# Experts: chosen tokens fetched by an indirect DMA, results added in place, weight rows dealt out in pairs, one more lasting place for weights

## Chip, cores and metric

One core of a Trainium2 chip runs the whole program. The metric is the device time of one execution in microseconds (us), the median of several runs. The profile comes from one further execution, and all rows below are of that one.

## What is computed

Two transformer blocks run one after the other on 512 tokens of width 1024. The change is about the experts at the end of the first block: 16 experts, each taking the 64 tokens that it rates highest, with three 1024x1024 float32 weight matrices per expert.

```python
def expert_choice_moe(h, w_router, w_gate, w_up, w_down):
    b_, length, _ = h.shape
    cap = EC_CAPACITY_FACTOR * length // N_EXPERTS          # 64
    aff = jax.nn.softmax((h @ w_router).astype(jnp.float32), axis=-1)
    gate, idx = lax.top_k(jnp.swapaxes(aff, 1, 2), cap)
    xe = h[bidx, idx]
    hid = jax.nn.silu(jnp.einsum("becd,edf->becf", xe, w_gate)) * jnp.einsum("becd,edf->becf", xe, w_up)
    ye = jnp.einsum("becf,efd->becd", hid, w_down) * gate[..., None].astype(h.dtype)
    return jnp.zeros_like(h).at[bidx, idx].add(ye)
...
x = x + g1 * y_x                                            # the token mixer's result
x = x + g2 * expert_choice_moe(modulate(rms_norm(x, norm2_g[l]), sh2, sc2), ...)
```

## The kernel before

The program is one stream per engine, laid out ahead of time by a scheduler: the order of the instructions on each engine is fixed, and an engine waits in order on semaphores.

The token mixer ends in `mix_out`, which adds its result to `X` (512 tokens as 4 blocks of 128 partitions, 1024 columns) and computes the router's logits. `router` makes the affinities `aff` and, for each expert, the place 1 to 64 of each chosen token (`sl`, 0 where it isn't chosen). `moe` then goes through 8 rounds `p`, two experts in each, one in each half of the 128 partitions:

- `prep(p)` fetches the chosen tokens by matrix multiplication. A one-hot matrix `D` of the 512 tokens by 128 places is made (L1069) and scaled by the tokens' rms factor (L1080); for each of 8 column chunks four matmuls of X by D (L1085) give the tokens already transposed, and ScalarE and VectorE scale and shift them into `xe` (L1087, L1090).
- three products, `G` (gate), `U` (up) and `Y` (down), of 32 matmuls each, 64 columns of the array for each expert (L1063; L1051 in the last round, where `gemm_parts` makes Y in three pieces of columns).
- between U and Y the hidden values `hs` are multiplied (L1128), transposed (`tp`, L1130) and copied to `hT` (`xh` in the profile, L1131, L1132).
- `back(p)` transposes a second one-hot D (L1099) to `oh` and picks the gate values with four matmuls (L1104).
- Y is scaled to `ye` (part of the tile `hy`, L1153) and split in a high and a low half `yh` (L1154, L1155); for each of 4 token blocks and 2 column pieces two matmuls (L1158, L1159) spread it back over the tokens, and VectorE adds that to `ACC` (L1164). In the last round X, to which GpSimd has added ACC (L1151), takes the sum.

The weights come in pieces of 1 MiB: two rows blocks of 128, for each partition two runs of 1024 floats, so 4 KB each. `mload` hands out places for them in a fixed cycle: 6 of kind x1, 3 raw, 3 hl (two halves of 512 KB), 3 x2. Before that cycle, 6 further places serve once (four in `rw1`, `rw2`, and two that become ACC afterwards): 21 pieces can be there when the first round begins. The transfers are issued by SyncE's queue (SP) in the order of use, and each waits until the matmuls on the piece that had its place are done. 192 pieces are needed in all. The last 8 pieces (12 transfers, in `gemm_parts`) have a list of their own: three places x2 and one of `rw2`, three times over.

```python
todo = (kinds[:6] + [(self.rw1, "rw2"), (self.rw2, "rw")] + kinds[6:] +
        [(self.rw1, "rw"), (self.rw2, "rw2")] + acc)
```

Of the kernel before, what the change touches and what calls it, by code (L numbers as in the profile page):

```python
# [20 lines left out]
def constants():  # L21
# [31 lines left out]
    iota = np.repeat(np.arange(1, 65, dtype=f)[None, :], 128, axis=0)  # L53
    return {
# [6 lines left out]
    }  # L61


class Build:
# [111 lines left out]
    def first_mixer(self):  # L176
# [32 lines left out]
        put("n2", I["norm2_g"][0].rearrange("(r p) -> r p", p=128), 8)  # L209
        put("lb", I["hg_lb_logits"].rearrange("a b (h p) -> (a b h) p", p=128), 16)  # L210
        put("hgn", I["hg_norm_g"][0].rearrange("(r p) -> r p", p=128), 4)
        self.prow = rows
# [9 lines left out]
        nc.vector.tensor_copy(self.pcol, tp[:, :128])  # L222
        cs = p1.tile([128, 8, 32], F32, name="cs")
# [157 lines left out]
        es1.close()  # L381
        esw = ExitStack()
# [20 lines left out]
    def ctx_part(self, cx, rest):  # L403
# [20 lines left out]
        def shift(i):  # L424
            for j, at in enumerate((0, 1, 2, 3)):
                if at == i:
                    self.mod_col(cx, pc, (self.sh2, self.sc2)[j // 2], 3 + j // 2, j % 2)
# [18 lines left out]
        nc.vector.scalar_tensor_tensor(self.sc2, self.sc2, 1.0, self.c("n2"), op0=ALU.add, op1=ALU.mult)  # L446
# [458 lines left out]
    def mod_col(self, pool, psp, out, wi, half, tag="mr"):  # L905

        nc = self.nc
        for s, row in self.mod_rows(pool, psp, wi, tag, (half,)):
            ps = psp.tile([128, 512], F32, name="mr", tag=tag, bufs=self.nmr)
            for k in range(4):  # L910
                nc.tensor.matmul(ps[:, 2 * k:2 * k + 2], row[:, k * 128:(k + 1) * 128], self.selc,
                                 start=True, stop=True)
            c = 8 * wi + 4 * s
            nc.vector.tensor_tensor(out[:, 4 * s:4 * s + 4], ps[:, :8].rearrange("p (k i) -> p k i", i=2)[:, :, 0],
                                    self.c("bmod")[:, c:c + 4], op=ALU.add)

    def mix_out(self, end):
# [3 lines left out]
        nc.sync.dma_start(wr, I["w_router"][0].rearrange("(k p) e -> p k e", p=128))  # L921
# [9 lines left out]
        def logits(n):  # L931
            for k in (2 * n, 2 * n + 1):
                tp = pp.tile([128, 512], F32, name="tp", tag="tp", bufs=2)
                for b in range(4):
                    nc.tensor.transpose(tp[:, b * 128:(b + 1) * 128], self.X[:, b, k * 128:(k + 1) * 128], self.ident)
# [26 lines left out]
    def router(self):  # L962

        nc, mo, ms, pp = self.nc, self.mo, self.ms, self.pmx
        iota = self.iota = ms.tile([128, 64], F32, name="iota")
        nc.sync.dma_start(iota, self.I["k_iota"])
        rs = self.rs = ms.tile([128, 4], F32, name="rs")
# [3 lines left out]
        e = self.aff = ms.tile([128, 4, 16], F32, name="aff")  # L971
# [32 lines left out]
    def moe(self):  # L1004
# [7 lines left out]
        todo = (kinds[:6] + [(self.rw1, "rw2"), (self.rw2, "rw")] + kinds[6:] +  # L1012
                [(self.rw1, "rw"), (self.rw2, "rw2")] + acc)

        def mload(src, last):
            if last == 2 and not self.tail:

                self.tail = True
                todo[:] = ["x2", "x2", "x2", (self.rw2, "rw2")] * 3
            if not todo:  # L1020
                todo.extend(k for k in kinds if not last or k != "hl")
            kind = todo.pop(0)
            shape = [128, src.shape[1], src.shape[2]]
# [12 lines left out]
            else:  # L1036
                pool, n = (self.mwx, 6) if kind == "x1" else (ms, 3)
                t = pool.tile(shape, F32, name="mwt", tag="mwt", bufs=n)
# [3 lines left out]
        def gemm_parts(ps, lhs, wa, wb):  # L1042

            ws = [w.rearrange("(k p) f -> p k f", p=128) for w in (wa, wb)]
            for y, c in zip(ps, parts):
                for kk in range(2):
                    tl = [mload(w[:, 4 * kk:4 * kk + 4, c], 2) for w in ws]
# [6 lines left out]
        def gemm(ps, lhs, wa, wb, last=0):  # L1054
            wa = wa.rearrange("(k p) f -> p k f", p=128)
            wb = wb.rearrange("(k p) f -> p k f", p=128)
            for kk in range(4):
                tl = [mload(w[:, 2 * kk:2 * kk + 2, :], last) for w in (wa, wb)]
# [8 lines left out]
        def onehot(p, tag, prev=None):  # L1067
            D = ms.tile([128, 4, 128], F32, name="D", tag=tag, bufs=1)
            ins = nc.vector.tensor_tensor(D.rearrange("p b (a s) -> p b a s", a=2),  # L1069
                                          self.iota.unsqueeze(1).unsqueeze(1).to_broadcast([128, 4, 2, 64]),  # L1070
                                          self.sl[:, :, 2 * p:2 * p + 2].unsqueeze(3).to_broadcast([128, 4, 2, 64]),
                                          op=ALU.is_equal)
            if prev:
                self.after(ins, prev)
            return D

        def prep(p):

            Ds = onehot(p, "Ds")
            nc.vector.tensor_tensor(Ds, Ds, self.rs.unsqueeze(2).to_broadcast([128, 4, 128]), op=ALU.mult)  # L1080
            xe = XE[p % 2]
            for k in range(8):
                ps = self.psmm()[:, :128]
                for b in range(4):
                    nc.tensor.matmul(ps, self.X[:, b, k * 128:(k + 1) * 128], Ds[:, b], start=(b == 0), stop=(b == 3))  # L1085
                if k % 2:
                    nc.scalar.activation(xe[:, k], ps, AF.Identity, bias=self.sh2[:, k:k + 1],  # L1087
                                         scale=self.sc2[:, k:k + 1])
                else:
                    ins = nc.vector.tensor_scalar(xe[:, k], ps, self.sc2[:, k:k + 1], self.sh2[:, k:k + 1],  # L1090
                                                  op0=ALU.mult, op1=ALU.add)
            return xe, ins

        def back(p, prev):

            D = onehot(p, "D", prev)
# [3 lines left out]
            oh = ms.tile([128, 512], F32R, name="oh", tag="oh", bufs=1)  # L1100
            nc.scalar.activation(oh, ps, AF.Copy)
            gps = self.psmm()
            for b in range(4):
                nc.tensor.matmul(gps[:, :16], D[:, b], self.aff[:, b], start=(b == 0), stop=(b == 3))  # L1104
            gc = ms.tile([128, 1], F32, name="gc", tag="gc", bufs=2)
            for a in range(2):
                nc.vector.tensor_copy(gc[64 * a:64 * a + 64], gps[64 * a:64 * a + 64, 2 * p + a:2 * p + a + 1])
            return oh, gc
# [3 lines left out]
        xe, ins = prep(0)  # L1112
        for p in range(8):
# [3 lines left out]
            if p == 0:  # L1117
# [3 lines left out]
                hs, ye = hy[:, 0], hy[:, 1]  # L1121
            nc.scalar.activation(hs, G, AF.Silu)
            U = pg.tile([128, 2, 512], F32, name="U", tag="gu", bufs=2)
            gemm(U, xe, wu[2 * p], wu[2 * p + 1], int(p == 7))
            oh, gc = back(p, ins)
            if p < 7:
                xe, ins = prep(p + 1)
            nc.vector.tensor_tensor(hs, hs, U, op=ALU.mult)  # L1128
            for k in range(8):
                nc.tensor.transpose(tp[:, k], hs[:, k * 128:(k + 1) * 128], self.ident)  # L1130
# [14 lines left out]
            yh = self.rw1.tile([128, 2, 1024], F32R, name="yh", tag="rw")  # L1145
            if p == 0:
                ACC = [pl.tile([128, 2, 1024], F32, name="acc", tag=t) for pl, t in acc]
                ACC = [ACC[b // 2][:, b % 2] for b in range(4)]
            elif p == 7:
                for b in range(4):  # L1150
                    nc.gpsimd.tensor_tensor(self.X[:, b], self.X[:, b], ACC[b], op=ALU.add)  # L1151
            for y, s in zip(Y, parts):
                nc.vector.scalar_tensor_tensor(ye[:, s], y, gc, self.g2[:, s], op0=ALU.mult, op1=ALU.mult)  # L1153
                nc.scalar.activation(yh[:, 0, s], ye[:, s], AF.Copy)  # L1154
                nc.vector.tensor_tensor(yh[:, 1, s], ye[:, s], yh[:, 0, s], op=ALU.subtract)  # L1155
                for b in range(4):
                    ps = self.psmm()[:, :s.stop - s.start]
                    nc.tensor.matmul(ps, oh[:, b * 128:(b + 1) * 128], yh[:, 1, s], start=True, stop=False)  # L1158
                    nc.tensor.matmul(ps, oh[:, b * 128:(b + 1) * 128], yh[:, 0, s], start=False, stop=True)  # L1159
                    if p == 0:  # L1160
                        nc.vector.tensor_copy(ACC[b][:, s], ps)
                    else:
                        d = ACC[b][:, s] if p < 7 else self.X[:, b, s]
                        nc.vector.tensor_tensor(d, ps, d, op=ALU.add)  # L1164
# [503 lines left out]
```

## Time and profile before

| what | value |
|---|---|
| median of three runs | 1828.63 us (1821.88 to 1828.9) |
| the profiled execution, its own time | 1826.09 us |
| its span, first to last instruction | 1824.3 us |
| mean granted TensorE clock | 0.975 of 2.4 GHz |
| TensorE (PE) busy | 1718.1 us, 94% |
| VectorE, ScalarE, GpSimd busy | 46%, 35%, 11% |
| moved from and to memory | 327.76 MB, 180 GB/s on average |

A busy share is an average over stages with different limits, so the table only tells that TensorE is seldom idle. "Busy" for matmuls is modelled from their pipelining. The experts run from about 637 us to 1151 us; the rows of that stretch are given further below.

### The profile page before, as it was taken

Reading aid. Unit: us, or ns where it says so; the run is one execution under the profiler, and the core shown is the slowest. Engines: PE = TensorE matmul, PEld = TensorE weight load, DVE = VectorE, ACT = ScalarE, POOL = GpSimd, SP = SyncE. Lnnn points to the kernel's source line nnn. Section 1 sums busy time; section 2 is a strip of 40 time slices with the busy share of each in tenths; the row PEclk is TensorE's granted clock in tenths of the full one; section 3 lists DMA queues with packets and bytes.
Section 4 is the critical chain, followed back from the end, with each engine's and each line's share of the span. In section 5 each row is a group of like instructions: output and inputs, shape, how many; then the busy total and the mean of one; then the engine's idle time right before and its main releaser. Section 6 shows DMA issues by size and latency. Waiting matters only on the chain.

```text
span 1824.3 us, 26988 instructions
## 1 busy us (share of the span) xinstructions
PE 1718.1 (94%) x11159; PEld 1251.9 (69%) x11159; DVE 842.7 (46%) x1613; ACT 631.1 (35%) x1098; POOL 198.3 (11%) x225
## 2 busy tenths in 40 slices
PE   5998888999999599999999999899999999999999
PEld 3986768776778553444334333697667989898989
DVE  5637898856334512212212221656774543434342
ACT  4627675566323210010000000555563241324131
POOL 0103343122110000000000001410221000000000
PEclk9999898999999799999999999999999999999999
DMA  9562111211568578999999996441002223323231
GB/s 309 181 210 70 48 47 43 70 36 35 211 215 300 189 291 324 407 409 380 395 373 364 407 386 229 140 162 47 24 24 70 73 90 93 107 78 116 70 116 47
DMA packets 177395, 327.76 MB, mean 180 GB/s; under 512 B 8580, under 2 KB 115816, under 8 KB 177272
## 3 DMA queue, kind: packets, MB, share of 16 engines
q1 hardware_dynamic: 176480, 325.44, 49.4%
q8 instruction: 88, 1.44, 0.3%
q10 hardware_dynamic: 744, 0.51, 0.1%
q14 instruction: 35, 0.29, 0.0%
q0 software_dynamic: 48, 0.08, 0.0%
HBM read 323.91 MB, written 2.10 MB: 179 GB/s over the span
## 4 chain that ended last, share of the span: by engine, by line
PE 63%; DVE 4%; ACT 1%; DMA 1%; issue 1%; POOL 0%; SPq 0%; DVEq 0%; ACTq 0%
PE mm L85 10%; PE mm L84 10%; PE mm L86 10%; PE G L1063 7%; PE U L1063 6%; PE Y L1063 5%; PE mm L1085 3%; PE po L1595 1%; PE mm L1158 1%; PE pt L1548 1%; PE mm L1159 1%; PE sc L1527 1%; PE sc L1528 1%; PE Y L1051 1%; PE hp L1450 0%
## 5 line engine op out<-in xcount | busy, mean ns | idle before, releaser
L76 ACT ACTIVATE whi<-wraw 128x1024 fp32r<-128x1024 f32 (+1 forms) x171 | 173.3, 1017 | 364.7 <-PE mm L84 176.8
L78 DVE TENSOR_TENSOR wlo<-wraw,whi 128x1024 fp32r<-128x1024 f32 (+1 forms) x171 | 208.1, 1218 | 122.4 <-ACT whi L76 121.6
L85 PE MATMUL mm<-whi,ul 128*128 128x256 f32 x512 | 144.3, 282 | 0.0
L84 PE MATMUL mm<-wlo,uh 128*128 128x256 f32 x512 | 143.2, 281 | 0.0
L86 PE MATMUL mm<-whi,uh 128*128 128x256 f32 x512 | 143.2, 281 | 0.0
L84 PE MATMUL mm<-HXl,whi 128*128 128x512 f32 x256 | 106.5, 416 | 0.0
L85 PE MATMUL mm<-HXh,wlo 128*128 128x512 f32 x256 | 105.4, 412 | 0.1
L86 PE MATMUL mm<-HXh,whi 128*128 128x512 f32 x256 | 105.2, 411 | 0.0
L84 PE MATMUL mm<-H,whi 128*128 128x512 f32 x256 | 99.7, 390 | 0.0
L86 PE MATMUL mm<-H,whi 128*128 128x512 f32 x256 | 99.7, 389 | 0.0
L85 PE MATMUL mm<-H,wlo 128*128 128x512 f32 x256 | 99.6, 389 | 0.0
L85 PEld LDWEIGHTS mm<-whi,ul 128*128 128x128 f32 x512 | 96.5, 188 | 1.0 <-DVE ul L1631 0.8
L84 PEld LDWEIGHTS mm<-wlo,uh 128*128 128x128 f32 x512 | 96.2, 188 | 0.2
L86 PEld LDWEIGHTS mm<-whi,uh 128*128 128x128 f32 x512 | 96.2, 188 | 0.0
L1085 PEld LDWEIGHTS mm<-D,X 128*128 128x128 f32 x512 | 61.8, 199 | 18.5 <-issue 15.4
L1640 DVE SCALAR_TENSOR_TENSOR X<-mm,r,X 128x256 f32<-128x256 f32 x64 | 30.9, 482 | 88.2 <-PE mm L86 88.2
L1085 PE MATMUL mm<-D,X 128*128 128x128 f32 x512 | 66.6, 287 | 2.8 <-DVE D L1080 1.8
L1151 POOL TENSOR_TENSOR X<-X,acc 128x1024 f32<-128x1024 f32 x4 | 9.3, 2364 | 533.6 <-issue 533.6
L1128 DVE TENSOR_TENSOR hy<-hy,U 128x1024 f32<-128x1024 f32 x8 | 9.8, 1221 | 124.4 <-PE U L1063 124.4
L1063 PE MATMUL Y<-mwt,xh 128*64 128x512 f32 x240 | 60.0, 594 | 5.4 <-DVE xh L1131 5.4
L1626 DVE TENSOR_SCALAR r<-mm 128x512 f32<-128x512 f32 x32 | 22.1, 691 | 85.3 <-PE mm L86 85.3
L1153 DVE SCALAR_TENSOR_TENSOR hy<-Y,gc,g 128x512 f32<-128x512 f32 (+1 forms) x17 | 11.6, 716 | 107.0 <-PE Y L1063 100.1
(541 smaller groups left out, 4180.0 us busy)
## 6 DMA issues: line engine op xcount, KB each, us to landing
mwt<-in_w_exp_gate_dram SPq DMA_DIRECT2D x41, 1024.0 KB, 8.9
mwt<-in_w_exp_up_dram SPq DMA_DIRECT2D x35, 1024.0 KB, 10.2
mwt<-in_w_exp_down_dram SPq DMA_DIRECT2D x33, 1024.0 KB, 12.4
wraw<-in_w_in_dram SPq DMA_DIRECT2D x29, 1024.0 KB, 6.6
wraw<-in_w_mod_dram SPq DMA_DIRECT2D x16, 1024.0 KB, 6.9
wraw<-in_w_up_dram SPq DMA_DIRECT2D x16, 1024.0 KB, 5.5
wraw<-in_w_down_dram SPq DMA_DIRECT2D x16, 1024.0 KB, 5.0
mwh<-in_w_exp_up_dram SPq DMA_DIRECT2D x30, 512.0 KB, 9.4
```

Of the source, the lines that this page charges most:

```text
L76: i1 = self.nc.scalar.activation(hi, src, AF.Copy)
L78: i2 = self.nc.vector.tensor_tensor(lo, src, hi, op=ALU.subtract)
L84: mm(ps, ah, bl, start=first, stop=False)
L85: mm(ps, al, bh, start=False, stop=False)
L86: mm(ps, ah, bh, start=False, stop=last)
L1051: nc.tensor.matmul(y[64 * a:64 * a + 64], lhs[:, k, 64 * a:64 * a + 64], tl[a][k4], start=(k == 0), stop=(k == 7))
L1063: nc.tensor.matmul(ps[64 * a:64 * a + 64, n], lhs[:, k, 64 * a:64 * a + 64], tl[a][k2][:, n * 512:(n + 1) * 512], start=(k == 0), stop=(k ...
L1085: nc.tensor.matmul(ps, self.X[:, b, k * 128:(k + 1) * 128], Ds[:, b], start=(b == 0), stop=(b == 3))
L1158: nc.tensor.matmul(ps, oh[:, b * 128:(b + 1) * 128], yh[:, 1, s], start=True, stop=False)
L1159: nc.tensor.matmul(ps, oh[:, b * 128:(b + 1) * 128], yh[:, 0, s], start=False, stop=True)
L1626: nc.vector.tensor_scalar(r, ps, 0.0, None, op0=ALU.max)
L1640: nc.vector.scalar_tensor_tensor(self.X[:, b, s], ps, r2[:, b:b + 1], self.X[:, b, s], op0=ALU.mult, op1=ALU.add)
```

## The change

Five things change in the experts, and their neighbours follow.

1. The sum of the mixer, X, is also written to memory (`XD`, in 4 pieces, on GpSimd's queue). For each round, `chosen(p)` multiplies the one-hot D by `aff`, which has two more columns now: the token's number and its rms factor. An indirect DMA on GpSimd's queue fetches the 128 rows of XD into `xg` (the first) or into `ye`, half of the tile `hy` (the other seven). `prep(p)` scales them (128x1024) and turns them by 8 transposes.
2. ACC is gone: the results are added to X directly. Rounds 0 and 1, 2 and 3, 4 and 5 are spread back together, with four matmuls in a row in one accumulation, so 8 additions for two rounds.
3. Weight rows are dealt out to the partitions in pairs: a partition holds rows 2p and 2p+1 of a block of 256, one run of 8 KB. The columns of X, `xg` and `hs` are taken with a step of 2 where they are transposed (`chunk`), and the per-column vectors (router, shift, scale) are loaded to match; for that, three small loads and two small transposes come in at the start of the program (`r256`, `pair`).
4. The cycle has one more lasting place, x3, so 16; the two that became ACC are gone, so 20 pieces can be there at the beginning.
5. The last 8 pieces have nine places instead of four: five of x1's six, x2's three, and one of `rw2`; each of their tiles comes in two transfers.

```diff
+def chunk(k):
+    return slice(k // 2 * 256 + k % 2, k // 2 * 256 + 256, 2)
...
+        for i, src in enumerate((I["b_mod"][0, 3072:4096], I["b_mod"][0, 4096:5120], I["norm2_g"][0])):
+            nc.scalar.dma_start(r256[4 * i:4 * i + 4], src.rearrange("(r p) -> r p", p=256))
...
+                if b == 3:
+                    nc.gpsimd.dma_start(self.XD.rearrange("(b p) f -> p b f", p=128)[:, :, s], self.X[:, :, s])
...
+        nc.gpsimd.tensor_copy(self.aff[:, :, 16], iota[:, 64:])
+        nc.gpsimd.tensor_copy(self.aff[:, :, 17], rs)
...
-        acc = [(self.mwx2, "acc0"), (self.mwx2, "acc1")]
-        kinds = ["x1"] * 6 + ["raw"] * self.nraw + ["hl"] * (self.nhl // 2) + ["x2"] * 3
+        kinds = ["x1"] * 6 + ["raw"] * self.nraw + ["hl"] * (self.nhl // 2) + ["x2"] * 3 + ["x3"]
+        place = {"x1": (self.mwx, "mwt", 6), "x2": (ms, "mwt", 3), "x3": (self.mwx2, "mwt", 1)}
...
-                todo[:] = ["x2", "x2", "x2", (self.rw2, "rw2")] * 3
+                todo[:] = ["x1", "x1", (self.rw2, "rw2"), "x2", "x2", "x2", "x1", "x1", "x1", "x1",
+                           (self.rw2, "rw2"), "x2"]
...
-            wa = wa.rearrange("(k p) f -> p k f", p=128)
-            wb = wb.rearrange("(k p) f -> p k f", p=128)
+            ws = [w.rearrange("(k p j) f -> p k j f", p=128, j=2) for w in (wa, wb)]
...
+        def chosen(p, xg):
+            D = onehot(p, "D")
+            ps = self.psmm()[:, :18]
+            for b in range(4):
+                nc.tensor.matmul(ps, D[:, b], self.aff[:, b], start=(b == 0), stop=(b == 3))
+            g = ms.tile([128, 18], F32, name="gs", tag="gs", bufs=2)
+            nc.vector.tensor_copy(g, ps)
+            at = ms.tile([128, 1], U32, name="at", tag="at", bufs=2)
+            nc.vector.tensor_copy(at, g[:, 16:17])
+            nc.gpsimd.indirect_dma_start(xg, None, self.XD, bass.IndirectOffsetOnAxis(ap=at, axis=0))
+            return xg, g
...
+        def prep(p, xg, g):
+            nc.vector.tensor_scalar(xg, xg, g[:, 17:18], None, op0=ALU.mult)
             xe = XE[p % 2]
-            for k in range(8):
-                ps = self.psmm()[:, :128]
-                for b in range(4):
-                    nc.tensor.matmul(ps, self.X[:, b, k * 128:(k + 1) * 128], Ds[:, b], start=(b == 0), stop=(b == 3))
+            for k0 in range(0, 8, 4):
+                ps = self.psmm()
+                for k in range(k0, k0 + 4):
+                    nc.tensor.transpose(ps[:, (k - k0) * 128:(k - k0 + 1) * 128], xg[:, chunk(k)], self.ident)
...
-        xe, ins = prep(0)
+        ch = chosen(0, ms.tile([128, 2, 1024], F32, name="xg", tag="rw")[:, 0])
+        xe = prep(0, *ch)
+        held = []
...
+            if p < 7:
+                ch = chosen(p + 1, ye)
...
-            yh = self.rw1.tile([128, 2, 1024], F32R, name="yh", tag="rw")
-            if p == 0:
-                ACC = [pl.tile([128, 2, 1024], F32, name="acc", tag=t) for pl, t in acc]
-                ACC = [ACC[b // 2][:, b % 2] for b in range(4)]
-            elif p == 7:
-                for b in range(4):
-                    nc.gpsimd.tensor_tensor(self.X[:, b], self.X[:, b], ACC[b], op=ALU.add)
+            yh = (ms if p % 2 else self.rw1).tile([128, 2, 1024], F32R, name="yh", tag="rw")
+            held.append((oh, yh))
...
+                if p in (0, 2, 4):
+                    continue
...
+                    parts_ = [(o, y[:, i, s]) for o, y in held for i in (1, 0)]
+                    for i, (o, v) in enumerate(parts_):
+                        nc.tensor.matmul(ps, o[:, b * 128:(b + 1) * 128], v, start=(i == 0), stop=(i == len(parts_) - 1))
+                    nc.vector.tensor_tensor(self.X[:, b, s], ps, self.X[:, b, s], op=ALU.add)
```

The scheduler places the new steps. On TensorE before, from the first U to the first Y (one-hot transposes L1099, gate values L1104, the fetch L1085, transposes of hs L1130):

```order
L1063 MATMUL U<-mwt,xe 64x512 x8
L1099 MATMUL mm<-ca,D 128x128 x4
L1104 MATMUL mm<-aff,D 128x16 x4
L1085 MATMUL mm<-D,X 128x128 x32
L1130 MATMUL tp<-ca,hy 128x128 x8
```

The same place now (L1148 one-hot transposes, L1132 transposes of the fetched tokens, L1181 those of hs, L1117 the matmuls of `chosen` for round 2; those for round 1 stand ahead of U):

```order
L1100 MATMUL U<-mwt,xe 64x512 x8
L1148 MATMUL mm<-ca,D 128x128 x4
L1132 MATMUL mm<-ca,hy 128x128 x8
L1181 MATMUL tp<-ca,hy 128x128 x8
L1117 MATMUL mm<-aff,D 128x18 x4
```

The 32 matmuls of the fetch have become 8 transposes, and the gate values have moved into `chosen`.

On TensorE now, the G of round 2, which stands for those of rounds 4 and 6 (L1209 spreads rounds 0 and 1 back, L1117 is `chosen` for round 3, L1132 the transposes of its tokens):

```order
L1100 MATMUL G<-mwt,xe 64x512
L1209 MATMUL mm<-yh,oh 128x512 x28
L1100 MATMUL G<-mwt,xe 64x512 x16
L1117 MATMUL mm<-aff,D 128x18 x4
L1148 MATMUL mm<-ca,D 128x128
L1100 MATMUL G<-mwt,xe 64x512 x7
L1148 MATMUL mm<-ca,D 128x128 x3
L1100 MATMUL G<-mwt,xe 64x512
L1132 MATMUL mm<-ca,hy 128x128 x8
L1100 MATMUL G<-mwt,xe 64x512 x7
```

Between the choice of the tokens and the transposes that need them stand 8 matmuls of G and 4 transposes.

On VectorE now, from the end of round 2 into round 3, which stands for rounds 4 and 5 as well (L1200 makes `ye` in the tile hy, L1202 its low half, L1127 scales the tokens that the indirect DMA has brought into hy):

```order
L1182 COPY xh<-tp 128x512
L1200 SCALAR_TENSOR_TENSOR hy<-Y,gc,g_4734 128x512 x2
L1202 TENSOR_TENSOR yh<-hy,yh 128x512
L1178 COPY gc<-gs 64x1 x2
L1202 TENSOR_TENSOR yh<-hy,yh 128x512
L1127 TENSOR_SCALAR hy<-hy,gs 128x1024
L1139 TENSOR_SCALAR xe<-mm,sc_695,sh_694 128x128 x4
```

The tokens of the next even round land in the tile that Y's result has just left, so their fetch waits for the end of Y and L1202.

## Rows read from the trace of the kernel before

**Rows 1.** Busy time by stretch: us, PE, PEld, DVE, ACT, POOL, clock, DMA share, GB/s.

```profile
687.28:745.55 58.27, 57.00 (x293) 25.71 (x293) 13.58 (x23) 5.28 (x9) 0.00 (x0) 1.00 0.89 342
...
939.04:1003.85 64.81, 61.70 (x292) 26.28 (x292) 13.61 (x23) 5.17 (x9) 0.00 (x0) 1.00 0.96 377
```

**Rows 2.** What SP's transfers waited for, 480 to 1160 us, the longest total.

```profile
SPq L1039 <- PE G L1063: 105.0, 34, 15.0
```

**Rows 3.** Chain that ended last, one early round and parts of later ones.

```profile
687.28 13.95 PE Y L1063 x64
...
720.93 13.73 PE U L1063 x63
735.25 0.80 PE mm L1104 x8
736.05 6.48 PE mm L1085 x56
...
869.95 15.53 PE Y L1063 x64
...
1000.70 1.23 DVE hy L1128
1001.98 1.11 PE tp L1130 x8
1003.11 0.70 DVE xh L1131
```

**Rows 4.** Chain that ended last, the last round.

```profile
1122.82 3.67 PE Y L1051 x16
...
1126.95 4.55 DMA mwt<-in_w_exp_down_dram
...
1138.25 6.15 DMA mwo<-in_w_exp_down_dram
...
1150.60 0.74 DVE X L1164 x2
```

**Rows 5.** Busy time by stretch: full DMA engines with runs of 4 KB and of 1 KB.

```profile
20.00:25.00 5.00, 5.00 (x45) 2.41 (x44) 3.11 (x6) 0.77 (x2) 0.00 (x0) 1.00 1.08 338
25.00:30.00 5.00, 4.83 (x36) 2.48 (x35) 3.66 (x8) 0.00 (x0) 0.00 (x0) 1.00 1.07 350
...
752.00:840.00 88.00, 83.91 (x410) 36.07 (x407) 21.78 (x37) 7.10 (x12) 0.00 (x0) 1.00 1.03 409
```

**Rows 6.** Costs of one: line, engine, operation, shapes, count, busy us, mean ns.

```profile
L1164 DVE TENSOR_TENSOR acc<-mm,acc 128x512 f32<-128x512 f32 x48 | 31.2, 686 | 17.3 <-PE mm L1159 17.3
...
L1154 ACT ACTIVATE yh<-hy 128x512 fp32r<-128x512 f32 x15 | 9.3, 630 | 108.6 <-DVE hy L1153 108.6
...
L1090 DVE TENSOR_SCALAR xe<-mm,sc,sh 128x128 f32<-128x128 f32 x16 | 6.6, 410 | 44.2 <-PE mm L1085 44.2
```

**Rows 7.** The only DMA on GpSimd's queue (80 KB): times in ns, then landing.

```profile
L539 POOL DMA_DIRECT2D levf<-in_k_lev_dram x1: 719/719/719, 131.1 to 131.1; - x1
...
DMA to landing us min/median/max: 5.1/5.1/5.1
```

**Rows 8.** DMA issues by kind: count, KB each, median us from issue to landing.

```profile
wraw<-in_w_exp_gate_dram SPq DMA_DIRECT2D x11, 1024.0 KB, 16.5
```

**Rows 9.** In order of time, the start: ScalarE and the wait that ends it.

```profile
8.63 1.06 ACT L256 ACTIVATE junk<-X 128x1024 f32<-128x1024 f32 x1
...
17.65 2.74 DVE L260 TENSOR_SCALAR X<-X,rs 128x1024 f32<-128x1024 f32 x4
17.68 0.18 PEld L298 LDWEIGHTS wm<-wmt,cs 128*32 128x32 f32 x2 [8.33 <-DVE rs L141]
```

**Rows 10.** In order of time, from the router to the first G.

```profile
637.30 0.69 DVE L1069 TENSOR_TENSOR D<-iota,sl 128x512 f32<-128x512 f32 x1
...
638.78 10.06 PE L1085 MATMUL mm<-D,X 128*128 128x128 f32 x64 [1.77 <-DVE D L1080]
```

**Rows 11.** A weight load's wait where the array changes between 64 and 128 columns.

```profile
PEld mm L1085 <- issue: 15.4, 19, 0.8
```

More of the change, by code (lines that the diff above doesn't have):

```diff
@@ L222, in first_mixer @@
         nc.vector.tensor_copy(self.pcol, tp[:, :128])
+        tp = pst.tile([128, 512], F32, name="tp", tag="tr", bufs=2)
+        for j in range(2):
+            nc.tensor.transpose(tp[:, 12 * j:12 * j + 12], r256[:, j::2], self.ident[:12, :12])
+        self.pair = p1.tile([128, 2, 12], F32, name="pair")
+        nc.vector.tensor_copy(self.pair, tp[:, :24].rearrange("p (j r) -> p j r", j=2))
         cs = p1.tile([128, 8, 32], F32, name="cs")
@@ L381, in first_mixer @@
         es1.close()
+        dp = self.es.enter_context(tc.tile_pool(name="xd", bufs=1, space=bass.MemoryType.DRAM))
+        self.XD = dp.tile([512, 1024], F32, name="XD")
         esw = ExitStack()
@@ L445, in ctx_part @@
         shift(3)
-        nc.vector.scalar_tensor_tensor(self.sc2, self.sc2, 1.0, self.c("n2"), op0=ALU.add, op1=ALU.mult)
+        pairs = lambda t: t.rearrange("p (k j) -> p k j", j=2)
+        nc.vector.scalar_tensor_tensor(pairs(self.sc2), pairs(self.sc2), 1.0, self.pair[:, :, 8:]
+                                       .rearrange("p j k -> p k j"), op0=ALU.add, op1=ALU.mult)
         nc.scalar.activation(KY, FR, AF.Sigmoid, scale=-1.0)
@@ L1022, in mload @@
             kind = todo.pop(0)
+            if len(src.shape) == 4:
+                pool, tag, n = kind + (None,) if isinstance(kind, tuple) else place[kind]
+                t = pool.tile([128, src.shape[1] * 2, src.shape[3]], F32, name="mwt", tag=tag, bufs=n)
+                for i in range(src.shape[1]):
+                    nc.sync.dma_start(t[:, 2 * i:2 * i + 2], src[:, i])
+                return [t[:, i] for i in range(t.shape[1])]
             shape = [128, src.shape[1], src.shape[2]]
@@ L1036, in mload @@
             else:
-                pool, n = (self.mwx, 6) if kind == "x1" else (ms, 3)
-                t = pool.tile(shape, F32, name="mwt", tag="mwt", bufs=n)
+                pool, tag, n = place[kind]
+                t = pool.tile(shape, F32, name="mwt", tag=tag, bufs=n)
                 nc.sync.dma_start(t, src)
@@ L1097, in back @@
+        def back(p):
+            D = onehot(p, "D")
             ps = self.psmm()
@@ L1099, in back @@
                 nc.tensor.transpose(ps[:, b * 128:(b + 1) * 128], D[:, b], self.ident)
-            oh = ms.tile([128, 512], F32R, name="oh", tag="oh", bufs=1)
+            oh = ms.tile([128, 512], F32R, name="oh", tag="oh", bufs=2)
             nc.scalar.activation(oh, ps, AF.Copy)
-            gps = self.psmm()
-            for b in range(4):
[L1104 to L1108, printed above, removed]
+            return oh
         wg, wu, wd = I["w_exp_gate"][0], I["w_exp_up"][0], I["w_exp_down"][0]
         XE = {0: self.xp.tile([128, 8, 128], F32, name="xe", tag="g1")}
-        xe, ins = prep(0)
+        ch = chosen(0, ms.tile([128, 2, 1024], F32, name="xg", tag="rw")[:, 0])
+        xe = prep(0, *ch)
+        held = []
         for p in range(8):
@@ L1124, in moe @@
             gemm(U, xe, wu[2 * p], wu[2 * p + 1], int(p == 7))
-            oh, gc = back(p, ins)
+            oh = back(p)
             if p < 7:
-                xe, ins = prep(p + 1)
+                xe = prep(p + 1, *ch)
+            gc = ms.tile([128, 1], F32, name="gc", tag="gc", bufs=2)
+            for a in range(2):
+                nc.vector.tensor_copy(gc[64 * a:64 * a + 64], gs[64 * a:64 * a + 64, 2 * p + a:2 * p + a + 1])
             nc.vector.tensor_tensor(hs, hs, U, op=ALU.mult)
             for k in range(8):
-                nc.tensor.transpose(tp[:, k], hs[:, k * 128:(k + 1) * 128], self.ident)
+                nc.tensor.transpose(tp[:, k], hs[:, chunk(k)], self.ident)
             nc.vector.tensor_copy(hT[:, 0:4], tp[:, 0:4])
```

83 lines of the change are left out of this document (40 added, 43 removed).

## The prediction

> **What bounds the kernel now.** I read the windows of the expert stretch first, one for each round from the start of a Y to the next Y. An early round takes 58.27 us and a late one 64.81 us, with TensorE busy 57.00 and 61.70 us of them, while the DMA engines stand at a share of 0.89 and 0.96 [rows 1]. So two limits lie side by side: TensorE's stream of work, and 24 MiB of weights for a round. Which of them gives way is told by the queue's own waits: the transfers on SP waited most of all for TensorE to be done with a place, 105.0 us for G alone [rows 2]. TensorE sets the pace, and the weights keep up with little to spare. The chain of waits agrees: through the rounds it runs over TensorE, with VectorE between U and Y [rows 3], and only in the last round over transfers, 4.55 and 6.15 us [rows 4]. From the first G (its fetch begins at 638.78 us and takes 10.06 us [rows 10], so 648.8) to the last addition to X (1150.60 + 0.74 [rows 4], so 1151.3) it is 502.5 us. I work out this stretch anew on both limits and take the longer.
>
> **TensorE's time, term by term.** I start from the early round of [rows 3], whose order of work is that of the new round 0.
>
> Products: G, U and Y keep their matmuls, 13.95 us for Y and 13.73 us for U [rows 3]; I take 13.75 for each of G and U.
>
> Fetch: U ends at 720.93 + 13.73 = 734.66 us and the next Y starts at 745.55 us [rows 1, 3], so 10.9 us between them. Of it the fetch itself is 6.48 us and the gate values 0.80 us [rows 3]. Now 8 transposes stand there; the 8 of hs take 1.11 us [rows 3]. What is left on the path is VectorE's: the product of hs 1.23 us, three scalings at 0.41 [rows 6], a one-hot 0.69 [rows 10], the copy 0.70 [rows 3], together 3.85, with hand-overs 4.1 us. In a late round, where the fetch stands elsewhere, U to Y is 1.23 + 1.11 + 0.70 with hand-overs 3.2 us [rows 3].
>
> Spreading back: from the end of Y (687.28 + 13.95 = 701.23) to the start of U (720.93) it is 19.7 us [rows 3]; less G that is 6.0 us, some 5.5 without the hand-over at U. Two rounds together need as many matmuls as before but half the additions: 8 of 0.69 us [rows 6] hide behind 32 matmuls of some 0.23 us, 7.4 us; ahead of them TensorE waits for the first yh (two steps of VectorE of 0.69 and one of ScalarE of 0.63 us [rows 6], less one matmul of G, 1.7 us). So 9.5 us for two rounds instead of 11.
>
> Changes of the array: in rounds 2 to 6 the transposes and `chosen` stand among the matmuls of G in three places. A weight load waited up to 0.8 us at each such change [rows 11]; three make 2.4 us in a round.
>
> The wait for the indirect DMA is the new term. No row shows one. The only DMA on GpSimd's queue landed 5.1 us after its issue with 80 KB [rows 7]. 512 KB take 1.3 us at 409 GB/s [rows 5], and 2.6 us if half the engines' time goes to the weights; I take 5.1 + 2.6 = 7.7 us. The bounds are 3.2 us shorter (at 4.5 us: the same landing without its 0.72 us of issue, nothing for the bytes) and, from the rows of weight transfers beside it, a median landing of up to 16.5 us [rows 8]. It is nearer the first, since the engine's queue is its own. Rounds 0 and 1 have all of U between choice and use, and hide it. In G of rounds 2, 4 and 6, 8 matmuls of G (3.4 us) and 4 transposes lie between: copy, one-hot and cast 1.1 us, landing 7.7, scaling 0.69 us (2.74 us for four [rows 9]) make 9.5 us, against some 4.5: a wait of 5 us, three times. In G of rounds 3 and 5 the fetch waits for Y's result to leave the tile hy (four steps of VectorE of 0.69 us as in [rows 6], two short copies and the hand-overs, 3.7 us), so its tokens are ready 3.7 + 7.7 + 0.7 = 12.1 us after Y; TensorE has 9 matmuls of G, 3.9 us: a wait of 8.2 us, twice. After the wait for the late Y the clock fell and its 64 rows took 15.53 us instead of 13.95 [rows 3]; I add 2 us to each of these two.
>
> The stretches: first G to first Y 13.9 + 2 (G now starts on an array that has rested, where the fetch used to come first) + 0.9 + 13.75 + 4.1 = 34.7. Round 0 to 1: 13.95 + 13.75 + 13.75 + 4.1 + 0.8 = 46.4. A late round without spreading: 13.95 + 27.5 + 3.2 + 0.55 for the one-hot + 0.8 + 1.1 + 2.4 = 49.6. Rounds ending on pairs: 49.6 + 9.5 + 5 = 64.1, three times; those between: 49.6 + 8.2 + 2 = 59.8, twice; the last but one, with a spread of its own and no fetch: 49.6 - 2.7 + 5.5 = 52.4. The last round took 1151.3 - 1122.8 = 28.5 us with 10.7 us of waits for transfers [rows 4], which the nine places remove if the queue never stands: 17.8. Sum 34.7 + 46.4 + 192.3 + 119.6 + 52.4 + 17.8 = 463 us.
>
> **The weights' time.** Full engines moved 409 GB/s with runs of 4 KB and 338 to 350 with runs of 1 KB [rows 5]: 160 ns and 47.6 ns for a run on one of 16 engines. The line through both gives 310 ns for 8 KB, 423 GB/s. I take that; the bounds are 409 (nothing) and 424. After 20 pieces that are there, 164 follow before the last eight: 134 in runs of 8 KB at 2.48 us, 30 of kind hl still in 4 KB at 2.56, seven fetches at 1.28, and the last 8 in runs of 2 and 1 KB, 23 us: 332 + 77 + 9 + 23 = 441. With 4 us until the first place is free and 6 from the last landing to the last addition it is 451 us, and 462 at 409 GB/s.
>
> A rule of the Trainium skill speaks against the long runs: "DMA: Bandwidth & Descriptors", Why small descriptors are slow, puts the overhead at about 3 bus cycles for a packet. By it an 8 KB run saves some 1% on 4 KB (an estimate from that page), 414 GB/s, and the weights' path would be 458 us. The two rates of [rows 5] show a dearer packet than that.
>
> So TensorE's 463 us is the longer by a little: a gain of 39.5 us in the stretch.
>
> **What lies around.** At the start ScalarE's second square, 1.06 us and 0.19 to read it [rows 9], now stands behind the exponential, and TensorE was waiting there for what follows it, 8.33 us [rows 9]: 1.3 us lost, 0 at best. Router to first G: before 638.78 + 10.06 - 637.30 = 11.5 us [rows 10]; now one-hot 0.7, four matmuls 1.7, copy, one-hot and cast 1.1, fetch 5.1 + 1.3 (the weights' queue is quiet then), scaling 0.7, four transposes and one scaling 1.5: 12.1, so 0.6 more, I take 1. The four writes of X (2 MB, 5.1 us) lie under `mix_out` and the router, whose chain on VectorE comes before their first use; without that cover they would cost their 5 us once. Taking the tokens' columns with a step of 2 as the transposes' weights is in no row: nothing, or at most a doubled load, 1.1 us for 8 transposes, 18 us over all rounds; I take nothing, since the transposes differ in nothing else, and keep 18 for the range.
>
> 1826.1 - 39.5 + 1.3 + 1 = 1789 us against the profiled execution. The median of the runs is 2.5 us above that one: 1791.5 us.
>
> **Rivals.** (a) The weights become the bound: the fetch lands in 4.5 us, the waits fall away, and the stretch takes 451 us: 1779.5 us. For it: the DMA share of 0.96 already. Against: it needs every fetch quick. (b) The waits are longer, or the strided transposes cost part of their 18 us: 10 us of landing make 5 x 2.3 = 12 us more, both together 1805 to 1820 us. (c) Slower than before: the fetch takes its turn behind the weights already queued on the engines and lands like them, 16.5 us after its issue [rows 8]. Then five waits in G grow by 8.8 us each, rounds 0 and 1 are still covered, and TensorE stands while the places are full, so nothing is hidden: +44 us, 1835.5 us. It decides from a landing of some 15 us on. For it: SP keeps several MiB issued ahead. Against: it is another queue, and [rows 7] landed beside SP's traffic in 5.1 us. The Trainium skill, "DMA: Bandwidth & Descriptors", Queues, rings and completion order, says that an engine goes round its queues packet by packet; by that rule (c) can't be, and no row here shows it under full load. (d) No change: the change does its fetch but TensorE, freed, meets weights that move no faster and places that are fewer at the start; by the 462 us above that cannot eat more than 1 us, so it needs (b) in full and a lost tail, 10.7 us: 1830 us.
>
> **Chances.** Forecast (1782 to 1803) 0.55, (a) 0.15, (b) 0.17, (c) 0.08, (d) 0.05. Likeliest 1791.5 us. The range runs from the weights' bound at its best, with the start's 1.3 us saved, 1774, to the worst of (b) with the strided transposes, 1823; (c) and most of (d) stay out. A measurement tells 0.5% (9 us) from no change: faster 0.87, same 0.05, slower 0.08.
>
> **What the profile will show.** A round of some 47 us first, then pairs of about 64 and 60; transposes of the fetch waiting for VectorE's scaling, and that for the DMA, 5 and 8 us; landing of the fetch near 8 us; full-engine rate of 420 or more; no wait for transfers in the last round. The prediction fails if the fetch lands past 12 us, if waits for weights appear in every G, or if the 8 transposes take over 2 us.

## The result, and the profile after

The changed kernel takes 1814.19 us in the median of 4 runs (1812.67 to 1816.36), against 1828.32 us before, now also in the median of 4 runs: a ratio of 0.9932, 95% interval 0.9907 to 0.9956. It is 14 us faster where 37 had been forecast. The profiled execution has a span of 1810.9 us, 13.4 less than before.

The stretch that the prediction reckoned, from the first G to the last addition to X, went from 502.5 us to 1139.17 - 649.74 = 489.4 us, where 463 had been forecast. What lies around it changed little: the first G starts 0.9 us later (2.3 had been forecast), and what follows the experts is 1.2 us shorter. So the whole error lies in the stretch. Its windows from one Y to the next, with the same columns as [rows 1]:

```profile
649.74:683.64 33.90, 33.49 (x166) 13.55 (x168) 6.74 (x16) 6.02 (x12) 0.98 (x1) 0.97 0.84 336
683.64:728.96 45.32, 44.86 (x217) 16.46 (x218) 8.40 (x17) 4.76 (x10) 0.95 (x1) 1.00 1.02 418
728.96:800.62 71.66, 61.62 (x263) 25.48 (x263) 15.84 (x30) 6.00 (x12) 0.95 (x1) 0.95 1.02 420
800.62:861.33 60.71, 49.28 (x212) 18.66 (x213) 7.21 (x13) 4.60 (x9) 0.95 (x1) 0.92 1.01 413
861.33:930.52 69.19, 59.23 (x261) 25.26 (x261) 15.69 (x29) 5.80 (x11) 0.95 (x1) 0.98 0.98 399
930.52:991.24 60.72, 49.09 (x213) 18.66 (x213) 7.22 (x13) 4.60 (x9) 0.95 (x1) 0.92 0.99 396
991.24:1057.48 66.24, 56.50 (x248) 23.70 (x249) 14.15 (x25) 5.20 (x10) 1.26 (x9) 0.97 0.98 405
1057.48:1113.13 55.65, 51.66 (x220) 18.93 (x221) 9.93 (x14) 3.47 (x6) 0.00 (x0) 0.97 0.88 338
1113.13:1139.20 26.07, 24.13 (x144) 13.71 (x144) 10.66 (x23) 4.86 (x9) 2.53 (x2) 1.00 0.59 179
```

Column by column: in the five windows from 728.96 us on TensorE is idle for 9.7 to 11.6 us each and its clock is below full, while the DMA engines are at a share of about 1. Two limits lie side by side, as before, and the share alone can't say which one gives way. TensorE's own waits can (engine, what waited, for what: us in total, times, longest):

```profile
PE mm L1132 <- DVE hy L1127: 33.4, 5, 9.4
PE tp L1181 <- DVE hy L1179: 8.3, 6, 1.4
PE mm L1209 <- DVE yh L1202: 7.0, 5, 2.2
```

In the whole list of the matmuls' waits in this stretch no transfer of weights stands; SP's transfers, in turn, still wait for TensorE, the answer to [rows 2]:

```profile
SPq L1076 <- PE G L1100: 103.3, 25, 33.6
```

So TensorE sets the pace, and stands still for 33.4 us at the transposes of the fetched tokens. The chain of waits shows what for, in the round that begins at 728.96 us (start, us, what; the trace has two records for a matmul of G, U or Y, so x64 stands for 32 matmuls, and two for one of L1117):

```profile
728.22 0.74 PE mm L1209 x2
728.96 11.30 PE Y L1100 x50
740.26 0.66 PE mm L1209 x2
740.92 3.15 PE Y L1100 x13
...
744.56 0.74 DVE hy L1200
...
746.73 8.72 PE mm L1209 x28
755.45 7.02 PE G L1100 x32
762.47 1.01 PE mm L1117 x8
...
765.12 8.50 DMA hy<-XD,at
...
774.45 1.98 PE mm L1132 x8
776.43 4.28 PE G L1100 x14
780.72 1.00 PE mm L1117 x8
...
782.72 0.59 PE mm L1148 x4
```

The fetch, 8.5 us from issue to landing, stands in the chain between the choice (L1117) and the transposes (L1132), inside G. The median landing of the seven fetches, by the page's DMA issues (count, median us), was forecast at 7.7 us:

```profile
hy<-XD,at POOLq DMA_INDIRECT x7, 8.7
```

What the clock did around these waits (windows, columns as above):

```profile
747.00:750.00 3.00, 3.00 (x8) 1.92 (x8) 1.72 (x3) 0.00 (x0) 0.00 (x0) 0.52 1.03 429
750.00:755.00 5.00, 5.00 (x21) 3.56 (x20) 3.26 (x5) 0.00 (x0) 0.00 (x0) 0.95 1.01 419
755.00:762.00 7.00, 7.00 (x34) 2.23 (x33) 0.89 (x2) 0.00 (x0) 0.00 (x0) 1.00 1.01 417
...
774.45:776.43 1.98, 1.98 (x10) 1.65 (x12) 0.41 (x1) 0.36 (x1) 0.00 (x0) 0.50 0.98 410
776.43:781.00 4.57, 4.57 (x18) 1.51 (x18) 1.14 (x3) 1.60 (x5) 0.00 (x0) 0.85 1.02 425
```

After 2.2 us of waiting for the first yh the clock was 0.52 (nearly all at the level of 1.2 GHz) for 3 us of spreading; after the wait of 4.73 us for the fetch it was 0.50 for the transposes and 0.85 for the G behind them.

The last round, in the chain of waits:

```profile
1113.13 7.11 PE Y L1088 x32
...
1125.25 1.88 PE Y L1088 x16
1127.13 0.90 PE mm L1209 x3
...
1132.35 1.89 PE Y L1088 x14
...
1134.80 1.16 PE tp L1255 x8
...
1138.43 0.74 DVE X L1210 x2
```

The two transfers of [rows 4] are gone from the chain, as forecast, but the round still takes 26.0 us. Over all its rows it is 13.9 us of Y, 4.0 us of spreading matmuls, and 8.1 us of VectorE's and ScalarE's steps, hand-overs and 1.2 us of transposes of the next part.

### The profile page after: what moved, and what is told of

Read it like the earlier page. It is cut to its first block, busy times and chain, and to the rows that moved or that the text cites. A ratio compares the mean times of both kernels' runs of the same rounds, so it can differ in the third digit from the quotient of the medians.

```text
span 1810.9 us, 26122 instructions
## 1 busy us (share of the span) xinstructions
PE 1667.5 (92%) x10713; PEld 1214.0 (67%) x10713; DVE 827.6 (46%) x1606; ACT 630.6 (35%) x1098; POOL 201.1 (11%) x235
## 4 chain that ended last, share of the span: by engine, by line
PE 56%; DVE 3%; DMA 3%; ACT 1%; issue 1%; POOL 0%; DVEq 0%; ACTq 0%
PE mm L92 9%; PE mm L91 9%; PE mm L93 9%; PE U L1100 6%; PE G L1100 6%; PE Y L1100 6%; DMA hy<-XD,at 2%; PE mm L1209 2%; PE po L1643 1%; PE pt L1596 1%; PE Y L1088 1%; PE sc L1575 1%; PE mm L1132 1%; PE sc L1576 1%; DVE hy L1179 1%
## 5 line engine op out<-in xcount | busy, mean ns | idle before, releaser
L1100 PE MATMUL Y<-mwt,xh 128*64 128x512 f32 x288 | 65.2, 607 | 4.2 <-issue 4.2
L1100 PE MATMUL G<-mwt,xe 128*64 128x512 f32 x240 | 62.6, 621 | 0.0
L1200 DVE SCALAR_TENSOR_TENSOR hy<-Y,gc,g 128x512 f32<-128x512 f32 (+1 forms) x17 | 11.6, 715 | 111.3 <-PE Y L1100 85.3
L91 PEld LDWEIGHTS mm<-HXl,whi 128*128 128x128 f32 x256 | 49.8, 194 | 12.1 <-issue 2.4
L92 PEld LDWEIGHTS mm<-HXh,wlo 128*128 128x128 f32 x256 | 49.7, 194 | 11.6 <-issue 2.3
```

What stands on the lines that cost most here:

```text
L91: mm(ps, ah, bl, start=first, stop=False)
L92: mm(ps, al, bh, start=False, stop=False)
L1100: nc.tensor.matmul(ps[64 * a:64 * a + 64, n], lhs[:, k, 64 * a:64 * a + 64], tl[a][k2][:, n * 512:(n + 1) * 512], start=(k == 0), stop=(k ...
```

## The experiments

Three questions: what the five waits are worth and whether the weights stand right behind them; what the long runs do; and what became of the last round and of spreading in pairs. Each was timed against the kernel before. Ratios below are to that kernel, and differences in us are between medians. The runs were timed apart, and the kernel before had medians of 1825.7 to 1828.3 us beside them, so a difference of 3 us between two runs proves little by itself; there the traces decide. The added place x3 and the sum without ACC were not tried by themselves.

**The transposes of the fetch behind U.** One order is added.

```diff
-        def prep(p, xg, g):
+        def prep(p, xg, g, behind=None):
...
-                    nc.tensor.transpose(ps[:, (k - k0) * 128:(k - k0 + 1) * 128], xg[:, chunk(k)], self.ident)
+                    ins = nc.tensor.transpose(ps[:, (k - k0) * 128:(k - k0 + 1) * 128], xg[:, chunk(k)], self.ident)
+                    if behind and k == k0:
+                        self.after(ins, behind)
...
-            gemm(U, xe, wu[2 * p], wu[2 * p + 1], int(p == 7))
+            last = gemm(U, xe, wu[2 * p], wu[2 * p + 1], int(p == 7))
...
-                xe = prep(p + 1, *ch)
+                xe = prep(p + 1, *ch, last)
```

> The changed kernel with one order added: the 8 transposes of the fetched tokens stand behind the last matmul of U on TensorE, where they stood in the middle of G, up to a round earlier. Theory A (TensorE's own stream is the bound, and it stands still while the indirect DMA lands): the five waits, 33.4 us on TensorE, go, the clock falls less often, and some 2 us for 8 transposes come back beside VectorE's product; the stretch from the first G to the last addition to X falls from 489 us to 455 to 465, the time to some 1785 us. Theory B (the weights are the bound by now and hide most of these waits: the DMA engines were at a share of 0.98 to 1.02 in rounds 1 to 6): waits for weights of over 15 us in all appear on TensorE, the stretch stays above 475 us and the time above 1800 us.

Measured: 1785.29 us, ratio 0.9785 (0.9767 to 0.9802), 29 us faster than the changed kernel. The stretch is 1111.77 - 649.42 = 462 us. TensorE's waits:

```profile
PE U L1100 <- DMA mwt<-in_w_exp_up_dram: 11.1, 10, 1.4
PE mm L1212 <- DVE yh L1205: 8.1, 5, 2.2
...
PE Y L1100 <- DMA mwt<-in_w_exp_down_dram: 3.9, 3, 1.4
```

Windows, of the same round as the third above and of the 360 us in the middle:

```profile
728.72:790.06 61.34, 57.45 (x260) 24.10 (x259) 14.19 (x26) 5.70 (x11) 0.94 (x1) 0.97 1.02 419
...
690.00:1050.00 360.00, 325.57 (x1465) 127.43 (x1462) 72.79 (x132) 31.83 (x56) 5.98 (x14) 1.00 1.02 419
```

Theory A gave the time, and theory B named what comes next: the five waits are gone, the round has shrunk from 71.7 to 61.3 us, and the clock of the middle is full (1.00; 0.95 in the changed kernel, and still 0.97 in this round), but with waits for weights of 20.5 us in all (the two rows above and three smaller ones of G) the weights now set the pace. The fetch itself still lands 8.6 us after its issue; it lies under U.

**Half of TensorE's work left out.**

```diff
-                for k2 in range(2):
+                for k2 in range(1):
...
-                                             tl[a][k2][:, n * 512:(n + 1) * 512], start=(k == 0), stop=(k == 7))
+                                             tl[a][k2][:, n * 512:(n + 1) * 512], start=(k == 0), stop=(k == 6))
```

> The changed kernel with every second step of the contraction of G, U and Y left out (rounds 0 to 7; the last Y keeps all), so that TensorE has half its matmuls in the experts while every byte of the weights still comes; the output is another one. It measures the weights' own path, which the prediction put at 451 us from the first G to the last addition. If that sum is right the stretch takes 445 to 456 us with TensorE waiting for transfers in every round; if the weights' path had been mis-sized (theory B in its strong form) it takes 465 us or more.

Measured: 1775.99 us; the stretch is 1103.24 - 649.53 = 453.7 us. TensorE waits most for the fetch, and for weights 46.8 us in all, the longest group of it here; the window of 410 us shows the DMA engines full all the while:

```profile
PE mm L1132 <- DVE hy L1127: 47.4, 7, 8.6
PE U L1100 <- DMA mwt<-in_w_exp_up_dram: 21.4, 20, 1.9
```

```profile
660.00:1070.00 410.00, 287.39 (x1000) 110.11 (x996) 81.45 (x147) 36.89 (x64) 8.39 (x15) 0.87 1.02 419
```

With the engines full the fetch's waits cost the weights nothing, so the weights' path had been sized rightly (451 us); 454 is a little too much for it, since it ends on TensorE's last round, in which the first piece of Y took 8.80 us at a lower clock, against 7.11 in the changed kernel. The kernel with late transposes is within 9 us of it.

**Runs of 4 KB again.** In three rearrangements of the weights (experts and router) "(k p j)" becomes "(k j p)"; columns and constants of the second norm are contiguous again.

```diff
-    return slice(k // 2 * 256 + k % 2, k // 2 * 256 + 256, 2)
+    return slice(k * 128, k * 128 + 128)
...
-            ws = [w.rearrange("(k p j) f -> p k j f", p=128, j=2) for w in (wa, wb)]
+            ws = [w.rearrange("(k j p) f -> p k j f", p=128, j=2) for w in (wa, wb)]
```

> The changed kernel without the pairs: the rows of a pair are 128 rows apart again, so a run is 4 KB, and the transposes take contiguous columns; all else is as in the changed kernel, the sizes of the transfers too. The full-engine rate falls from some 421 to some 409 GB/s. Theory A: TensorE sets the pace; the time stays within 5 us, or falls by up to 6 us since the 8 transposes of the fetch, 1.98 us with a step of 2, become some 1.1 us. Theory B: the 187 MB of the stretch take 458 us in place of 443, and the time rises by 10 to 15 us.

Measured: 1807.42 us, ratio 0.9898 (0.9881 to 0.9915), so 6.8 us faster than the changed kernel: the long runs cost time here. The rate of full engines did fall, to 409 GB/s from 418 to 420 in the second and third window of the changed kernel, but over the middle as a whole the changed kernel had moved no more (408 GB/s):

```profile
690.00:1050.00 360.00, 314.48 (x1376) 123.72 (x1374) 65.74 (x121) 30.57 (x53) 5.98 (x14) 0.95 1.03 409
```

The row of its DMA issues for the fetch (count, median us to landing), and TensorE's waits:

```profile
hy<-XD,at POOLq DMA_INDIRECT x7, 7.5
```

```profile
PE mm L1131 <- DVE hy L1126: 27.5, 5, 8.0
```

The fetch landed 1.2 us earlier, and TensorE stood 5.9 us less for it. That suggests that the packets beside the fetch are what counts, but the transposes differ as well. Not all of the 6.8 us is the fetch: by the starts of the Ys the five rounds with a wait are 4.2 us shorter together, and the last but one, which has no fetch, 1.9 us. Its Y, in the changed kernel and here:

```profile
1057.48 15.67 PE Y L1100 x64
```

```profile
1055.29 13.97 PE Y L1099 x64
```

The clock read 0.62 in the first 4.5 us of the former and 1.00 in the latter, behind the same work and waits; why, no run shows.

**Contiguous transposes beside runs of 8 KB.**

```diff
-                    nc.tensor.transpose(ps[:, (k - k0) * 128:(k - k0 + 1) * 128], xg[:, chunk(k)], self.ident)
+                    nc.tensor.transpose(ps[:, (k - k0) * 128:(k - k0 + 1) * 128], xg[:, k * 128:(k + 1) * 128], self.ident)
```

> The changed kernel with runs of 8 KB, but the transposes of the fetched tokens take contiguous columns (they then do not fit the rows of the weights, so the output is another one). It parts the two sides of the 6.8 us that runs of 4 KB saved. Theory L: the fetch landed in 7.5 us beside packets of 4 KB and 8.7 us beside packets of 8 KB, which is 1.2 us in each of five waits, 6 us; then this kernel gains only 0.5 us in each fetch that TensorE stands for, 0 to 3 us in all. Theory S: the step of 2 cost those 6 us; then this kernel gains 5 to 7 us.

Measured: 1814.97 us, ratio 0.9938 (0.9918 to 0.9959): no change from the changed kernel, and a landing of 8.6 us. TensorE's waits for it are 32.8 us, 0.6 less. Theory L stands, theory S falls.

**Late transposes and runs of 4 KB.** Both edits together.

> Runs of 4 KB with contiguous transposes, as in the run with runs of 4 KB, together with the transposes of the fetch behind U. In the changed kernel the long runs cost 6.8 us, because TensorE set the pace there. With the waits gone the weights set it, at 419 GB/s with runs of 8 KB. Theory: now the long runs pay: at 409 GB/s the 425 us in which the engines are full become 435, so it is 8 to 12 us slower than the kernel with the late transposes alone, some 1795 us. Rival: contiguous transposes are worth as much here as there, so it is 3 to 7 us faster, 1780 us.

Measured: 1795.71 us, ratio 0.9832 (0.9812 to 0.9852), 10.4 us slower than the late transposes alone. The middle of the stretch:

```profile
690.00:1050.00 360.00, 322.74 (x1444) 120.97 (x1442) 66.26 (x123) 30.55 (x54) 5.97 (x14) 1.00 1.03 409
```

The long runs turn from a loss of 6.8 us, some 4 of them at the fetch, into a gain of 10.4 us once the weights set the pace.

**The old places for the last transfers.**

```diff
-                todo[:] = ["x1", "x1", (self.rw2, "rw2"), "x2", "x2", "x2", "x1", "x1", "x1", "x1",
-                           (self.rw2, "rw2"), "x2"]
+                todo[:] = ["x2", "x2", "x2", (self.rw2, "rw2")] * 3
```

> The changed kernel with the old list of places for the last 12 transfers (four places in turn, not nine). Theory A: the last round had waits for transfers in the kernel before, but TensorE's and VectorE's work of spreading back lay under them, so that taking the waits away bared it; with the old list the last round takes 28 to 29 us against 26, and the time rises by only 2 to 3 us. Rival, as predicted: the whole 10.7 us of those waits was the gain, so the time rises by 8 to 11 us.

Measured: 1817.47 us, ratio 0.9957 (0.9941 to 0.9972), 3.3 us slower than the changed kernel, near theory A and far from the rival. Its last round takes 1142.2 - 1112.9 = 29.3 us. The chain of its last round has a transfer again, and in the middle of it, but TensorE's own waits there show only 1.8 us of it:

```profile
1119.24 4.31 DMA mwt<-in_w_exp_down_dram
```

```profile
PE Y L1087 <- DMA mwt<-in_w_exp_down_dram: 1.8, 1, 1.8
```

**The kernel before with the new places.** The same edit the other way round, in the kernel before.

> The kernel before with only the new list of places for the last 12 transfers. The prediction took the 10.7 us of TensorE's waits for transfers in the last round as the gain. Theory A: the work of spreading back lay under them, so that the last round falls from 28.5 to 25 or 26 us and the time by 2 to 4 us. Rival: it falls by 9 to 11 us.

Measured: 1823.92 us, ratio 0.9980 (0.9967 to 0.9993), 2.9 us faster than the kernel before. Its last round, from Y to the last addition to X, takes 1149.4 - 1124.2 = 25.2 us in place of 28.5, with no transfer in the chain. The new places are worth some 3 us, not 10.7.

**Every round spread at once.**

```diff
-                if p in (0, 2, 4):
-                    continue
...
-            if p not in (0, 2, 4):
-                held = []
+            held = []
```

> The changed kernel, but every round spreads its own result back to X at once (two matmuls a block and an addition), where rounds 0 to 5 did it in pairs with four matmuls a block. The pairs cost 12.3 us of the path for two rounds (10.1 us for 32 matmuls and 2.2 us of waiting for the first yh), 9.5 had been reckoned, and 11 were spent before. Theory A: single spreading costs 11 us for two rounds, so the stretch changes by -4 to +2 us, apart from what the order of the fetch does to its waits. Rival: the pairs save 1.5 us for two rounds, as predicted, and the time rises by 5 us.

Measured: 1822.37 us, ratio 0.9977 (0.9967 to 0.9986), 8.2 us slower. Theory A falls on this point. By the starts of its Ys two rounds take 118.5, 132.8 and 132.2 us, against 117.0, 129.9 and 127.0 us in pairs, so pairs save 1.5 to 5.3 us, though they cost more than reckoned. TensorE stands less for the fetch here, 29.9 us, but two of the Ys take 15.67 us at a lower clock, 1.7 us more each. How the difference divides between the spreading, the clock and the places of the fetch in G, which move with it, stays open.

**Late transposes, every round spread at once.**

> The kernel with the late transposes, but every round spreads its own result back at once. In the changed kernel this cost 8.2 us, with TensorE setting the pace. The stretch of the kernel with the late transposes is 462 us, and with half of TensorE's matmuls left out 454 us, so there the weights set it nearly everywhere. Theory: spreading in pairs is hidden there, and the time stays within 3 us of 1785 us. Rival: TensorE's stream still counts in full, so it is 6 to 10 us slower, 1791 to 1795 us.

Measured: 1785.21 us, ratio 0.9774 (0.9756 to 0.9792): the same as with pairs. TensorE's waits for weights fall from 20.5 to 13.4 us: with the weights as the bound, the 8 us are hidden.

## Why the prediction was right in direction and wrong in size

The direction, the bound and the mechanism were right: TensorE's path was the longer one, the weights' path was forecast at 451 us and took 454 at most, and the fetch, put too early in TensorE's order, made five waits. The waits were even sized well: forecast three of 5 and two of 8.2 us, 31.4 in all; measured 4.7, 9.2, 5.1, 9.4 and 4.9 us, 33.4 in all, with a landing of 8.7 us against 7.7. For the three waits of 5 us that is in part luck: from the choice to the transposes it took 11.0 us, not 9.5 (763.48 to 774.45 us in the chain above), but 6.2 us of other work and a short wait lay between, not 4.5. What failed is the sizing of TensorE's own sum, in three places and by 26 us together. By stretch, forecast and measured: to the first Y 34.7 and 33.9; round 0 to 1 46.4 and 45.3; three rounds ending on pairs 192.3 and 207.1; the two between 119.6 and 121.4; the last but one 52.4 and 55.7; the last 17.8 and 26.0. (Two of the sum's terms don't follow from their parts: 7.4 and 1.7 us of spreading make 9.1, not 9.5, and a late round adds up to 49.5 us, not 49.6; and nothing shown leads to the lower end of the range, 1774.)

**The last round (8.2 us).** The step that failed is "10.7 us of waits for transfers [rows 4], which the nine places remove". 4.55 and 6.15 us in [rows 4] are the time from issue to landing of two transfers that the chain runs through, not the time that TensorE stood for them. Its own waits in the last round of the kernel before say so:

```profile
PE tp L1130 <- DVE hy L1128: 1.4, 1, 1.4
PE mm L1158 <- DVE yh L1155: 1.2, 1, 1.2
PE Y L1051 <- DMA mwt<-in_w_exp_down_dram: 1.0, 2, 0.8
...
PE Y L1051 <- DMA mwo<-in_w_exp_down_dram: 0.4, 1, 0.4
```

For transfers that is 1.4 us in all; the rest of the 10.7 lay beside Y and spreading. The two exchanges of places, in either kernel, gave 2.9 and 3.3 us.

**The rounds ending on pairs (14.8 us in three).** Three terms of the sum fell short.

- Spreading. Two rounds were taken as 9.5 us. In the chain above it is 0.74 us ahead of Y, in the window before, and 0.66 inside it, then 2.2 us of waiting for yh and 8.72 us: 12.3. The later two pairs take 9.8 us each from the end of Y to G (875.3 to 885.14 and 1005.2 to 1015.03 us) and 1.3 us for four matmuls ahead, which stand in the G of the round before. In the three windows that is 11.6, 9.8 and 9.8, 2.7 us too much in all. In the first, the matmuls behind the wait ran at half clock.
- The clock after a fetch. The sum added 2 us to each of the two rounds with long waits and nothing to these three. But after waits of 5 us, too, the 8 transposes took 1.98 us, against 1.22 for the 8 of hs, which stand behind waits of 1.4 us and ran at full clock (798.57 us); and the 13 or 14 records of G behind them took 4.28, 4.09 and 3.68 us, where 0.219 us each (7.02 us for 32) would make 2.8 to 3.1. That is 0.8 and some 1.0 us a round, 5.3 in three.
- The choice of tokens. The sum gave each round one choice, 0.8 us, and 0.55 us of one-hot transposes. Two of these three windows hold two choices of 1.0 us and 1.4 us of such transposes, the third one of 1.0 and 0.8, and in each TensorE waits 0.87 us behind the first choice for VectorE: some 7 us, about what was left of the 14.8.

The rounds between hold no choice at all, and only so, by luck, came out within 1.8 us though their waits were 2.2 us longer than forecast.

**The last but one (3.3 us).** Its Y ran at a lower clock (15.67 us against 13.95), which in the run with runs of 4 KB it did not, and its spreading from the end of Y, less the G in between, is 7.4 us where 5.5 had been put.

**The long runs.** 423 GB/s was the forecast, and the 360 us in the middle of the run with late transposes show 419, with some pieces still in 4 KB, against 409. But their use was put down for the weights alone, and their price was missed: fetches landed in 8.5 to 8.9 us (medians) in the seven kernels with runs of 8 KB and in 7.5 us in both kernels with 4 KB. The difference agrees with the 150 ns by which a run of 8 KB takes longer than one of 4 KB in the prediction's arithmetic, times the 8 rows that each of 16 engines fetches: 1.2 us.

That is as if each row waited for one run of weights, and the single DMA packets that the traces keep agree with it. In the last six fetches of the changed kernel, sixteen rows, as many as there are engines, start every 0.40 to 0.47 us in the median (0.16 for a row and 0.31 for a run of 8 KB), and 128 rows over 3.5 to 3.9 us with 115 to 137 runs of weights among them; in the same six of the run with runs of 4 KB it is every 0.32 us and 2.4 to 2.8 us. The one fetch of the run with late transposes that met only runs of 4 KB (issued at 923.14 us) took 2.6 us. On quiet engines it was 2.0 us, and the first row started 1.75 us after the issue, where it was 4.1 to 4.2 us beside either kind of run. The Trainium skill, "DMA: Bandwidth & Descriptors", Queues, rings and completion order, says that an engine goes round its queues packet by packet, a packet being some 9 to 17 descriptors as a rule. The traces agree with the turns, and rival (c), a landing of 16.5 us behind the queued weights, did not come; but the turns here were of about one run each. The traces kept don't name the engine of a packet, so the turns are read from these times and counts.

**The rivals.** (b) was in the right direction, but for the wrong reason: the transposes with a step of 2 cost nothing that showed in the time, and the landing was 1.0 us longer than taken, not 2.3. The weights become the bound, as in (a), only when the transposes stand late: 462 us for the stretch, with some 454 as the floor, and the fetch doesn't land sooner. Of (d) the lost tail came true for the most part.

## What to carry to other kernels

A new wait can be cheaper to move than to shorten: the fetch still takes 8.6 us, yet with its first reader placed behind U it is covered, and the gain grows from 14 to 42 us (a ratio of 0.9785). A duration of a transfer in the chain is from issue to landing; before it is booked as a gain, read how long the engine itself stood for it. Here bigger packets helped when the stream was the bound, and hurt the transfer that shared the engines and was waited for: the kernel with the long runs was 6.8 us slower in one order of work and 10.4 us faster in the other.

## What the runs showed of the hardware

A fetch of 128 rows of 4 KB by indirect DMA landed 4.3 us after its issue on quiet engines, 7.5 us beside a full stream in runs of 4 KB and 8.5 to 8.9 us beside runs of 8 KB; a longer run on the other queue delayed each row by about its own length. After a wait of TensorE of 2.2 us the clock read 0.52 in the 3 us behind it; in the run with runs of 4 KB, after 3.62 us, it read 1.00 for 1.1 us of transposes and 0.55 in the 3.4 us behind them. A load of 128 columns with a step of 2 as weights took 209 ns in the median at full clock, against 141 ns contiguous, and 8 such transposes 1.22 us against 1.09, too little to show in the time.
